# Pinning ScalarE's splits of the experts' weights in the order of use, in a two-layer hybrid encoder

## The chip, the cores and the metric

The kernel runs on one core of a Trainium2 chip. The metric is the device time of one execution in microseconds; the median of three runs is compared.

## What is computed

Two encoder layers work on 256 tokens of width 1024. Each layer has a token mixer (three parallel head groups behind one input projection), a cross-attention into 256 memory tokens, and a channel mixer; each is followed by a residual and a layer norm. The channel mixer of layer 0 is a dense SwiGLU. That of layer 1 is a mixture of 8 experts, of which each token takes 2:

```python
def moe_swiglu(x, w_router, w_gate, w_up, w_down):
    logits = (xt @ w_router)
    top_logit, top_e = lax.top_k(logits, TOP_K)          # 2 of 8
    top_w = jax.nn.softmax(top_logit, axis=-1)
    ...
    def expert_block(args):
        xs, e = args
        hdn = jax.nn.silu(xs @ w_gate[e]) * (xs @ w_up[e])   # 1024 -> 3584
        return hdn @ w_down[e]                               # 3584 -> 1024
```

All is float32. The experts' weights are 8 x 3 x 1024 x 3584 floats, 352 MB, and every one of them is read once.

## The kernel before

**A load and its splits.** `wload` (L293) fetches one piece of a weight matrix, 128 x 2048 floats or 1 MB, by one DMA on SP's queue into a raw tile `wr`. Then it splits the piece for exact products in a faster format: ScalarE copies it, rounded, to `wh` (L313), and VectorE subtracts, `wl = wr - wh` (L317). Both work in two parts of 128 x 1024. In layer 1's experts nothing of this goes to GpSimd. Raw tiles come from a ring of nine buffers, `wh` and `wl` from a ring of four: the split of a load must wait until TensorE is done with the load four before it, and the DMA of a load until TensorE and VectorE are done with the one nine before it.

**An expert in chunks.** `expert_run` (L1367) goes through the eight experts, and for each through seven chunks of 512 hidden columns. A chunk takes six loads. In the program's order these are gate halves g0 and g1 and up halves u0 and u1 (`gate_up`), and then the two down halves d0 and d1 of the chunk before (`flush`, `down`). I write g0 to d1 for them in what follows. TensorE's work on a chunk is: the gate product, four transposes of the hidden tile of the chunk before (`ps_hT`, L1430), the up product, and the two down products into `ps_ye`.

**Two ways to multiply.** `products` (L1372) branches on how many tokens the expert has. Over 64 tokens it runs `passes`: three matmuls a tile, `wh` and `wl` against the split activations (L1377 to L1379). Up to 64 it runs `paired`: one float32 matmul a tile, straight from the raw tile `wr` (L1385), with 64 rows for each of two tiles, which are added up by one more matmul, the fold (L1402). The fold takes `fe`, ScalarE's copy of the product's bank (L1401): the fold of up stands behind the down products, ahead of the next chunk's gate product. The branch is taken on the chip, so the splits are made for every expert, and are read only by those that run `passes`. In the trace these are experts 0, 6 and 7; experts 1 to 5 run `paired`. A matmul block of either way keeps its `wh` and `wl` until the block ends.

**ScalarE's other work in a chunk.** `fe` for gate and for up, the silu `hs` (L1423; VectorE multiplies it with up, L1424, and TensorE transposes it), and from the transposes `hw` (L1434) and `hh` (L409); VectorE makes `hl` (L409). Once an expert there are the gather of the next expert's tokens (`rows`, `xg`, `gw`) and the combine of the finished one (`yh` on ScalarE, `yl` and the sums into `x` on VectorE).

**What sets the order.** No order is written down for the engines. A scheduler takes the program, simulates it, and fixes the order of each engine's instructions from when they could start in that simulation and from priorities; `wload` gives its splits a priority of their own. Each engine then runs its instructions strictly in that order, and an instruction that waits holds up all that stand behind it.

Of the kernel before, what the change touches and what calls it, by code (L numbers as in the profile page):

```python
# [14 lines left out]
AF = mybir.ActivationFunctionType  # L15
# [137 lines left out]
def _offsets():  # L153
    out = {}
    for name, tiles in _tiles().items():
        at = 0
        for t in tiles:
            out[(name,) + t] = at
            at += P * t[2] * t[4]
    return out  # L160
# [3 lines left out]
def tile_encoder(ctx: ExitStack, tc: tile.TileContext, a: dict, out: bass.AP, cw: dict):  # L164
    nc = tc.nc
    V, A, G, T, SY = nc.vector, nc.scalar, nc.gpsimd, nc.tensor, nc.sync
# [28 lines left out]
    def rotate(ring):  # L195
        ring.append(ring.pop(0))
        return ring[-1]
# [92 lines left out]

    where = _offsets()

    def wload(name, i, k0, n0, c0, n1, late=(), whole=False):  # L293

        n = n0 * n1
        W = rotate(parts)
        raw = rotate(raws).tile([P, 2048], F32, name="wr")
        at = where[name, i, k0, n0, c0, n1]
        last_load[:] = [SY.dma_start(raw[:, :n], a[name][at:at + P * n].rearrange("(p n) -> p n", p=P))]
        h = W.tile([P, 2048], F32R, name="wh")  # L300
        l = W.tile([P, 2048], F32R, name="wl")
        c = n // pieces[0]

        if not late and gate[0] <= 0 < gate[0] + GATED:
            late = ln_end
        gate[0] -= 1
        with ExitStack() as es:
            for i in late:
                es.enter_context(tc.issue_after(i.ins))
            es.enter_context(tc.high_priority(offset=WP if in_mixer[0] else WQ))  # L310
            g = n * (GQ - GP[layer[0]]) // GQ if in_mixer[0] else n
            for s in (slice(j, j + c) for j in range(0, n, c)):
                A.activation(h[:, s], raw[:, s], AF.Copy)  # L313
                s0, s1 = s.start, s.stop
                if s0 < g:
                    m = slice(s0, min(s1, g))
                    V.tensor_sub(l[:, m], raw[:, m], R_(h[:, m]))  # L317
                if s1 > g:
                    m = slice(max(s0, g), s1)
                    G.tensor_sub(l[:, m], raw[:, m], R_(h[:, m]))  # L320
        v = lambda t: t[:, :n].rearrange("p (a b) -> p a b", a=n0)
        return (v(h), v(l), v(raw)) if whole else (v(h), v(l))
# [114 lines left out]
    def mixer(l, xh, xl, kctx):  # L437
        wi = ("w_in", l)
        with tc.tile_pool(name=f"mx{l}", bufs=1, reuse_waits="tile") as M, ExitStack() as mctx:
# [323 lines left out]
            if l == 0:  # L763
                next(pf)
                load_first()
            run(pf)
            wh, wl = wload(*wi, 0, KT, 4 * AW, 24)
            pb = bank(psb, "pb", "ps_bd")
            for k in range(KT):
# [855 lines left out]
```

## Time and profile before

| | us |
|---|---|
| median of 3 runs (lowest, highest) | 1989.45 (1986.8, 1990.65) |
| the profiled execution | 1993.32 |
| its span (first to last instruction) | 1991.5 |
| from the silu of expert 0's first chunk to that of expert 1's | 959.9 to 1089.7 |
| the same for experts 1 to 5, 35 chunks | 1089.7 to 1699.6 |
| the same for experts 6 and 7, to the last silu | 1699.6 to 1957.4 |

The profile is one execution. For each engine it gives busy time and idle time and, for the idle time, what ended it. A group's name reads out<-in by the program's names, after the engine and the line. The windows view cuts the span into stretches and gives busy time and number of instructions of each engine, then the clock granted to TensorE as a share of full speed, the busy share of the 16 DMA engines and the rate in GB/s. A silu (L1423) marks a chunk: from one to the next is a chunk's period.

### The profile page before, as it was taken

Reading aid. Unit: us, or ns where it says so; the run is one execution under the profiler, and the core shown is the slowest. Engines: PE = TensorE matmul, PEld = TensorE weight load, DVE = VectorE, ACT = ScalarE, POOL = GpSimd, SP = SyncE. Lnnn points to the kernel's source line nnn. Section 1 sums busy time; section 2 is a strip of 40 time slices with the busy share of each in tenths; the row PEclk is TensorE's granted clock in tenths of the full one; section 3 lists DMA queues with packets and bytes.
Section 4 is the critical chain, followed back from the end, with each engine's and each line's share of the span. In section 5 each row is a group of like instructions: output and inputs, shape, how many; then the busy total and the mean of one; then the engine's idle time right before and its main releaser. Section 6 shows DMA issues by size and latency. Waiting matters only on the chain. (4 is left out here: it accounts for less than half of the span.)

```text
span 1991.5 us, 29272 instructions
## 1 busy us (share of the span) xinstructions
PE 1739.0 (87%) x11084; PEld 1221.9 (61%) x11084; DVE 1551.0 (78%) x2175; ACT 1294.4 (65%) x2071; POOL 258.3 (13%) x248
## 2 busy tenths in 40 slices
PE   6889999999969889996999888888888888998985
PEld 5768778899967677785776333332333334676764
DVE  6887665755488866656778989999998889878775
ACT  4755444555437644453778887888988788777673
POOL 4545210000045452101000000000000000000000
PEclk8988999999989879997999999999999989999998
DMA  6321345555323221650789998999999899888782
GB/s 214 111 97 66 110 179 199 184 181 188 116 75 126 85 100 65 254 192 20 293 318 348 388 347 337 376 366 374 375 380 362 320 359 369 336 310 331 277 304 84
DMA packets 71281, 473.76 MB, mean 238 GB/s; under 512 B 8768, under 2 KB 12224, under 8 KB 15936
## 3 DMA queue, kind: packets, MB, share of 16 engines
q1 hardware_dynamic: 70384, 466.09, 62.9%
q10 hardware_dynamic: 720, 5.24, 0.7%
q8 instruction: 119, 1.95, 0.4%
q14 instruction: 58, 0.48, 0.1%
HBM read 470.26 MB, written 1.05 MB: 237 GB/s over the span
## 5 line engine op out<-in xcount | busy, mean ns | idle before, releaser
L317 DVE TENSOR_TENSOR wl<-wr,wh 128x1024 fp32r<-128x1024 f32 (+3 forms) x950 | 975.4, 1077 | 142.2 <-ACT wh L313 137.2
L313 ACT ACTIVATE wh<-wr 128x1024 fp32r<-128x1024 f32 (+2 forms) x984 | 852.8, 937 | 150.6 <-PE ps_ye L1379 48.1
L1385 PE MATMUL ps_gu<-wr,gw 128*64 128x512 f32 x1120 | 291.3, 631 | 0.1
L1385 PEld LDWEIGHTS ps_gu<-wr,gw 128*64 128x64 f32 x1120 | 95.9, 144 | 150.3 <-issue 142.8
L1402 PE MATMUL ps_gu<-fe,fold 128*64 128x512 f32 x146 | 88.1, 688 | 70.3 <-ACT fe L1401 70.3
L1385 PE MATMUL ps_ye<-wr,hw 128*64 128x512 f32 x560 | 148.2, 596 | 0.1
L1378 PE MATMUL ps_gu<-wl,xg 128*128 128x512 f32 x336 | 134.4, 400 | 11.3 <-DVE wl L317 11.3
L1377 PE MATMUL ps_gu<-wh,xg 128*128 128x512 f32 x336 | 137.1, 408 | 8.2 <-DVE m L1311 5.1
L320 POOL TENSOR_TENSOR wl<-wr,wh 128x384 fp32r<-128x384 f32 (+6 forms) x68 | 103.7, 1544 | 291.3 <-ACT wh L313 290.9
L1549 POOL TENSOR_TENSOR x<-x,lp 128x512 f32<-128x512 f32 x1 | 1.8, 1819 | 1058.8 <-ACT x L1548 1058.8
L1379 PE MATMUL ps_gu<-wh,xg 128*128 128x512 f32 x336 | 133.5, 397 | 0.0
L1434 ACT ACTIVATE hw<-ps_hT 128x512 f32<-128x512 f32 x56 | 33.5, 598 | 117.4 <-PE ps_hT L1430 117.4
L1258 PE MATMUL ps_gu<-xTl,wh 128*128 128x256 f32 x352 | 99.0, 281 | 0.0
L1259 PE MATMUL ps_gu<-xTh,wl 128*128 128x256 f32 x352 | 98.8, 281 | 0.0
L1257 PE MATMUL ps_gu<-xTh,wh 128*128 128x256 f32 x352 | 98.7, 282 | 0.0
L1402 PEld LDWEIGHTS ps_gu<-fe,fold 128*64 128x64 f32 x146 | 16.2, 145 | 125.7 <-ACT fe L1401 117.4
L1385 PEld LDWEIGHTS ps_ye<-wr,hw 128*64 128x64 f32 x560 | 49.9, 136 | 69.9 <-issue 66.7
L1377 PEld LDWEIGHTS ps_gu<-wh,xg 128*128 128x128 f32 x336 | 64.7, 192 | 28.1 <-ACT wh L313 7.4
L1378 PEld LDWEIGHTS ps_gu<-wl,xg 128*128 128x128 f32 x336 | 64.6, 192 | 27.6 <-DVE wl L317 14.5
L1379 PEld LDWEIGHTS ps_gu<-wh,xg 128*128 128x128 f32 x336 | 64.5, 192 | 14.2
L1377 PE MATMUL ps_ye<-wh,hh 128*128 128x512 f32 x168 | 67.5, 402 | 3.9 <-ACT wh L313 3.3
L409 DVE TENSOR_TENSOR hl<-ps_hT,hh 128x512 fp32r<-128x512 f32 x56 | 38.5, 688 | 39.0 <-ACT hh L409 38.8
(469 smaller groups left out, 3744.9 us busy)
## 6 DMA issues: line engine op xcount, KB each, us to landing
wr<-in_moe_wg_dram SPq DMA_DIRECT2D x112, 1024.0 KB, 7.3
wr<-in_moe_wu_dram SPq DMA_DIRECT2D x112, 1024.0 KB, 7.7
wr<-in_moe_wd_dram SPq DMA_DIRECT2D x112, 1024.0 KB, 7.6
wr<-in_w_in_dram SPq DMA_DIRECT2D x16, 1024.0 KB, 4.9
wr<-in_ffn_wg_dram SPq DMA_DIRECT2D x11, 1024.0 KB, 4.9
wr<-in_ffn_wu_dram SPq DMA_DIRECT2D x11, 1024.0 KB, 4.9
wr<-in_ffn_wd_dram SPq DMA_DIRECT2D x11, 1024.0 KB, 4.9
wr<-in_xk_dram SPq DMA_DIRECT2D x8, 1024.0 KB, 4.9
```

The costliest lines, as they stand in the source:

```text
L313: A.activation(h[:, s], raw[:, s], AF.Copy)
L317: V.tensor_sub(l[:, m], raw[:, m], R_(h[:, m]))
L320: G.tensor_sub(l[:, m], raw[:, m], R_(h[:, m]))
L409: return A.activation(h, ps, AF.Copy), V.tensor_sub(l, ps, R_(h))
L1257: T.matmul(ps[:, g], wh[:, k, fs], xh[:, k, :], start=k == 0, stop=False)
L1258: T.matmul(ps[:, g], wh[:, k, fs], xl[:, k, :], start=False, stop=False)
L1259: T.matmul(ps[:, g], wl[:, k, fs], xh[:, k, :], start=False, stop=k == KT - 1)
L1377: T.matmul(out, h[:, k], wh, start=b, stop=False)
L1378: T.matmul(out, h[:, k], wl, start=False, stop=False)
L1379: T.matmul(out, l[:, k], wh, start=False, stop=z)
L1385: T.matmul(out[f * HALF:f * HALF + HALF], hw[:, k, :HALF], w, start=ws[j][5], stop=ws[j + 1][6], skip_group_check=True)
L1402: return lambda: T.matmul(pt[:HALF], fold[e], fe, start=False, stop=True, skip_group_check=True)
```

## The change

`wload` gets a helper, `in_turn`. For the loads of the experts (`whole=True`) it ties each ScalarE part of a split to the part before it, in the order in which the program makes them. The tie is one between two instructions of one engine, so it carries no semaphore: it only forbids the scheduler another order.

```diff
+    split = []
+
+    def in_turn(i):
+
+        if split:
+            tc.add_manual_dep(i.ins, split[-1].ins.name, mybir.DependencyInfo(
+                mybir.DependencyClass.NoSync, mybir.DependencyReason.DATA), reason="in_turn")
+        split[:] = [i]
...
             for s in (slice(j, j + c) for j in range(0, n, c)):
-                A.activation(h[:, s], raw[:, s], AF.Copy)
+                act_i = A.activation(h[:, s], raw[:, s], AF.Copy)
+                if whole:
+                    in_turn(act_i)
```

Up to the experts all engines' orders are the same as before, and so are all instructions in number and kind. In 40 of the 56 chunks ScalarE split u0 ahead of g0 before, and in 14 right behind g0; now it stands behind g1 in all. Lines behind the helper are 9 to 11 further down in the changed kernel (L313 is L322, L1401 is L1412).

ScalarE in the third chunk of expert 1 (the place of rows 4 below), from the split of the second down half, 11566, to the next `hw`; 11596 and 11604 are g0 and g1 of the fourth chunk, 11648 and 11656 its u0 and u1, `fe_11528` and `hs_11592` are the third chunk's copy of up and its silu. Before:

```order
L313 ACTIVATE wh_11568<-wr_11566 128x1024 x2
L1393 UNCONDITIONAL_BRANCH x2
L313 ACTIVATE wh_11650<-wr_11648 128x1024 x2
L313 ACTIVATE wh_11598<-wr_11596 128x1024 x2
L1401 ACTIVATE fe_11528<-ps_gu_11477 128x512
L1423 ACTIVATE hs_11592<-ps_gu_11425 128x512
L313 ACTIVATE wh_11606<-wr_11604 128x1024 x2
L1393 UNCONDITIONAL_BRANCH x2
L313 ACTIVATE wh_11658<-wr_11656 128x1024 x2
L1434 ACTIVATE hw_11705<-ps_hT_11700 128x512
```

Now:

```order
L322 ACTIVATE wh_11568<-wr_11566 128x1024 x2
L1404 UNCONDITIONAL_BRANCH x2
L322 ACTIVATE wh_11598<-wr_11596 128x1024 x2
L1412 ACTIVATE fe_11528<-ps_gu_11477 128x512
L1434 ACTIVATE hs_11592<-ps_gu_11425 128x512
L322 ACTIVATE wh_11606<-wr_11604 128x1024 x2
L322 ACTIVATE wh_11650<-wr_11648 128x1024 x2
L1404 UNCONDITIONAL_BRANCH x2
L322 ACTIVATE wh_11658<-wr_11656 128x1024 x2
L1445 ACTIVATE hw_11705<-ps_hT_11700 128x512
```

The split of u0 moved from ahead of g0, `fe` and the silu to behind g1, so `fe` stands behind one split and not two.

VectorE at the same place, from g0 or u0 to the down half d0 (11711). Before:

```order
L317 TENSOR_TENSOR wl_11651<-wr_11648,wh_11650 128x1024 x2
L317 TENSOR_TENSOR wl_11599<-wr_11596,wh_11598 128x1024 x2
L1393 UNCONDITIONAL_BRANCH
L317 TENSOR_TENSOR wl_11607<-wr_11604,wh_11606 128x1024 x2
L1393 UNCONDITIONAL_BRANCH
L1424 TENSOR_TENSOR hs_11592<-hs_11592,ps_gu_11477 128x512
L317 TENSOR_TENSOR wl_11659<-wr_11656,wh_11658 128x1024 x2
L409 TENSOR_TENSOR hl_11708<-ps_hT_11700,hh_11707 128x512
```

Now:

```order
L328 TENSOR_TENSOR wl_11599<-wr_11596,wh_11598 128x1024 x2
L1404 UNCONDITIONAL_BRANCH
L328 TENSOR_TENSOR wl_11607<-wr_11604,wh_11606 128x1024 x2
L328 TENSOR_TENSOR wl_11651<-wr_11648,wh_11650 128x1024
L1404 UNCONDITIONAL_BRANCH
L328 TENSOR_TENSOR wl_11651<-wr_11648,wh_11650 128x1024
L1435 TENSOR_TENSOR hs_11592<-hs_11592,ps_gu_11477 128x512
L328 TENSOR_TENSOR wl_11659<-wr_11656,wh_11658 128x1024 x2
L420 TENSOR_TENSOR hl_11708<-ps_hT_11700,hh_11707 128x512
```

The subtractions follow ScalarE's new order; the multiplication of the silu stands behind the same six of them as before.

ScalarE at the end of expert 1, where its result is scaled (`yh_12501`, `yh_12513`) before the next expert's first chunk (g0 12530, u0 12582, u1 12590). Before:

```order
L313 ACTIVATE wh_12584<-wr_12582 128x1024 x2
L313 ACTIVATE wh_12532<-wr_12530 128x1024 x2
L1472 ACTIVATE yh_12501<-ps_ye_11358,gs_12497 128x512
L1472 ACTIVATE yh_12513<-ps_ye_11359,gs_12497 128x512
L313 ACTIVATE wh_12592<-wr_12590 128x1024 x2
L1401 ACTIVATE fe_12424<-ps_gu_12373 128x512
L1423 ACTIVATE hs_12526<-ps_gu_12321 128x512
```

Now:

```order
L322 ACTIVATE wh_12532<-wr_12530 128x1024 x2
L1483 ACTIVATE yh_12501<-ps_ye_11358,gs_12497 128x512
L1483 ACTIVATE yh_12513<-ps_ye_11359,gs_12497 128x512
L1412 ACTIVATE fe_12424<-ps_gu_12373 128x512
L1434 ACTIVATE hs_12526<-ps_gu_12321 128x512
```

Both up splits moved behind the silu here. Beside this, three smaller things move. The split of d0 stands ahead of `hw` and `hh` in 31 chunks now, in 9 before. On TensorE, eight chunks had the first down product ahead of the up product; it stands behind it now, as in all others. On SP's queue eight pairs of gate loads and one pair of down loads change places with each other.

## Rows read from the trace of the kernel before

**Rows 1.** The page's first lines: span, busy time and share of each engine.

```profile
span 1991.5 us, 29272 instructions
...
PE 1739.0 (87%) x11084; PEld 1221.9 (61%) x11084; DVE 1551.0 (78%) x2175; ACT 1294.4 (65%) x2071; POOL 258.3 (13%) x248
```

**Rows 2.** Windows of the expert stages; after the engines: granted clock, DMA share, GB/s.

```profile
core 0: us, PE busy (x) PEld busy (x) DVE busy (x) ACT busy (x) POOL busy (x), PEclk, DMA share, GB/s
...
959.90:1089.70 129.80, 120.27 (x517) 92.19 (x518) 103.30 (x99) 98.61 (x124) 0.00 (x0) 0.96 0.85 319
1089.70:1699.60 609.90, 516.57 (x2125) 201.28 (x2125) 559.47 (x561) 510.83 (x646) 0.00 (x0) 0.96 0.95 363
1699.60:1957.40 257.80, 236.65 (x1016) 185.56 (x1015) 205.01 (x199) 185.57 (x231) 0.00 (x0) 0.98 0.81 304
```

**Rows 3.** Waits in 1090 to 1700 us: waiter, releaser, total us, times, longest.

```profile
PE ps_gu L1402 <- ACT fe L1401: 70.3, 35, 2.8
...
DVE wl L317 <- ACT wh L313: 26.8, 51, 1.4
...
ACT wh L313 <- PE ps_ye L1385: 24.5, 23, 1.7
```

**Rows 4.** Timeline of ScalarE in expert 1: start, length, instruction, idle before.

```profile
1116.88 2.01 ACT L313 ACTIVATE wh<-wr 128x1024 fp32r<-128x1024 f32 x2
1119.90 3.90 ACT L313 ACTIVATE wh<-wr 128x1024 fp32r<-128x1024 f32 x4 [1.00 <-PE ps_ye L1385]
1123.70 0.58 ACT L1401 ACTIVATE fe<-ps_gu 128x512 f32<-128x512 f32 x1
1124.18 0.58 ACT L1423 ACTIVATE hs<-ps_gu 128x512 f32<-128x512 f32 x1
1124.65 3.89 ACT L313 ACTIVATE wh<-wr 128x1024 fp32r<-128x1024 f32 x4
1129.46 0.60 ACT L1434 ACTIVATE hw<-ps_hT 128x512 f32<-128x512 f32 x1 [0.92 <-PE ps_hT L1430]
```

**Rows 5.** Timeline of TensorE's matmuls at the same place.

```profile
1117.44 0.64 PE L1385 MATMUL ps_ye<-wr,hw 128*64 128x512 f32 x1
...
1117.92 3.64 PE L1385 MATMUL ps_ye<-wr,hw 128*64 128x512 f32 x15
1124.33 1.07 PE L1402 MATMUL ps_gu<-fe,fold 128*64 128x512 f32 x2 [2.77 <-ACT fe L1401]
1124.84 3.99 PE L1385 MATMUL ps_gu<-wr,gw 128*64 128x512 f32 x16
1128.76 0.66 PE L1430 MATMUL ps_hT<-consts,hs 128*128 128x128 f32 x4
1129.35 3.65 PE L1385 MATMUL ps_gu<-wr,gw 128*64 128x512 f32 x16
```

**Rows 6.** Timeline of VectorE at the same place.

```profile
1115.60 4.74 DVE L317 TENSOR_TENSOR wl<-wr,wh 128x1024 fp32r<-128x1024 f32 x4
1120.98 7.12 DVE L317 TENSOR_TENSOR wl<-wr,wh 128x1024 fp32r<-128x1024 f32 x6 [0.65 <-ACT wh L313]
1128.02 0.68 DVE L1424 TENSOR_TENSOR hs<-hs,ps_gu 128x512 f32<-128x512 f32 x1
```

**Rows 7.** Windows of single chunks, from silu to silu; columns as in rows 2.

```profile
1124.18:1140.10 15.92, 13.15 (x56) 4.90 (x56) 15.13 (x15) 14.00 (x19) 0.00 (x0) 0.99 1.00 399
...
1176.76:1194.40 17.64, 14.85 (x56) 5.92 (x56) 15.30 (x15) 14.03 (x19) 0.00 (x0) 0.90 0.94 352
...
1266.80:1281.60 14.80, 13.88 (x60) 5.16 (x60) 14.66 (x15) 13.88 (x19) 0.00 (x0) 1.00 0.97 374
1281.60:1300.10 18.50, 15.29 (x68) 5.75 (x68) 16.69 (x17) 16.87 (x24) 0.00 (x0) 1.00 0.99 381
...
1739.34:1758.30 18.96, 17.50 (x76) 13.84 (x76) 15.27 (x15) 14.03 (x18) 0.00 (x0) 1.00 0.88 330
```

**Rows 8.** Waits of TensorE in 1699.6 to 1957.4 us; columns as in rows 3.

```profile
PE ps_gu L1378 <- DVE wl L317: 9.1, 8, 1.1
...
PE ps_gu L1377 <- ACT wh L313: 2.5, 8, 0.3
PE ps_ye L1377 <- ACT wh L313: 2.1, 1, 2.1
```

## The prediction, made before the changed kernel was run

> **What bounds the kernel now.** I began with the page's totals: TensorE is busy for 87% of 1991.5 us, VectorE for 78% [rows 1]. Such shares are means over stages, and the change touches one stage only, so the next view was the windows of the three expert stages [rows 2]. Experts 1 to 5, the ones with few tokens, take 609.9 us. There TensorE is busy for 516.6 us, but VectorE for 559.5 us and the DMA engines for 95%. Experts 0 and 6 to 7 are the reverse: TensorE 120.3 of 129.8 us and 236.7 of 257.8 us, with DMA at 85% and 81%. So there are two cases.
>
> The waits of the first case name one culprit [rows 3]: TensorE waited 70.3 us, in 35 waits over 35 chunks, for `fe`, ScalarE's copy of the up product, which the fold needs. The timelines of one chunk show why. TensorE ends the up product and starts the down products at 1117.4; they end at 1117.92 + 3.64 = 1121.6, and then it idles for 2.77 us until `fe` [rows 5]. The up product had been ready for 6 us by then, but ScalarE first sat idle for 1.00 us until TensorE was done with the first down half, then ran four split parts, 3.90 us, and only then `fe` [rows 4]. By the order of ScalarE these four parts are u0 and g0, u0 first. The buffer of u0's split is the one that d0 holds, so u0 waits for the down product, and g0 and `fe` stand behind it though they wait for nothing. This is a ring: up product, first down half, u0, g0, `fe`, fold, gate product, transposes, up product. Its period is 15.92 us in that chunk [rows 7].
>
> VectorE is close behind. In the same chunk it is busy for 15.13 of the 15.92 us [rows 7], and its only idle stretch there is 0.65 us, ahead of the six subtractions that follow the late splits [rows 6]. Over the stage it idled for 609.9 - 559.5 = 50 us, 26.8 of them in waits for splits [rows 2, 3].
>
> **The change part by part.**
>
> *ScalarE's own work* neither grows nor shrinks: the tie adds no instruction and no semaphore.
>
> *u0 behind g0, `fe` and the silu, few tokens.* In the chunk of rows 4, d1's split ends at 1116.88 + 2.01 = 1118.9. g0 needs the buffer of the last chunk's u0, free since 1117.4; so it runs to 1120.9, and `fe` starts there and not at 1123.70. It is done at 1121.5, when the down products end (1121.6): the 2.77 us are gone. TensorE's own ring is then 15.92 - 2.77 = 13.15 us, which is its busy time in that row.
>
> That isn't what a chunk will take, because VectorE needs 15.13 us and ScalarE 14.00. So the bound passes to VectorE, or to the DMA. What is late next is the multiplication of the silu, which still stands behind six subtractions. Two ends for the stage follow. If VectorE keeps the idle time that it has now in an ordinary chunk, 15.92 - 15.13 = 0.79 us, 35 chunks take 559.5 + 28 = 587 us, a gain of 23. If it gets down to that of the chunk at 1266.8, 14.80 - 14.66 = 0.14 us, they take 559.5 + 5 = 564, a gain of 45. That chunk is a preview: there TensorE ran the first down half ahead of the up product, so u0's buffer was free early, and the period was 14.80 us. The DMA gives a third figure. The stage moves 609.9 us x 363 GB/s = 221 MB; at the 381 GB/s that the chunk at 1281.6 shows with a share of 0.99, so at 385 if it were 1.00, this is 575 us, a gain of 35. I take 30: two limits that lie this close are seldom both reached.
>
> Chunks that are longer today give most of it. The one at 1176.8 has the same work, but TensorE's clock was granted at 0.90 over it, it was busy for 14.85 us, and 14.85 + 2.77 gives its 17.64 us [rows 7]. Without the wait such a spell lies under VectorE's 15.3 us: 2 us each. At the ends of experts, where u1 stood ahead of `fe` too, the copy comes another 2 us earlier.
>
> *u0 later, many tokens.* Here TensorE reads the splits. A chunk takes 18.96 us with 17.50 busy [rows 7], and the waits of experts 6 and 7 that splits cause are 9.1 + 2.5 + 2.1 = 13.7 us [rows 8]. They have the same cause: g0 is split behind u0, which waits for the down product's end, so the gate product finds `wl` of g0 unfinished. With g0 free to start when the up product ends, some 5.6 us ahead of its use (the down products lie between, about a third of the chunk's 17.5 us of matmuls), both ScalarE's 2.0 and VectorE's 2.4 us fit in. Expert 0 has the same order; by its idle time, 129.8 - 120.3, I give it a third as much as 6 and 7 together, 5. The bounds are 0 and 19; I take 15, because VectorE's 15.3 and the DMA's 0.88 leave room in a 17.5 us chunk [rows 7].
>
> *What could cost.* u0's split waits for the end of the first down half, and u1, d0, `hw` and the gate's `fe` are queued behind it. From the up product's end, ScalarE reaches u0 after g0, `fe`, the silu and g1, 2.0 + 0.6 + 0.5 + 1.9 = 5.0 us; the first down half ends after about 2.5 us [rows 4, 5]. So it doesn't wait. d0's split now stands ahead of `hw` in 31 chunks: 2.0 us, of which ScalarE has 0.92 us idle at that place [rows 4], and `hw` is wanted only behind the up product, 3.65 us after the transposes [rows 5]. I cost it at nothing; if the cover is gone it is the slower rival below. The eight chunks that lose their early down product lose nothing, since g0 no longer waits for it. The swaps on SP's queue put loads back into the order of use: nothing.
>
> **The sum.** 30 + 15 = 45 us off the profiled execution's 1993.3 gives 1948. The median of the runs is 1989.45, 3.9 us lower, so the forecast is 1944.
>
> **The rivals.**
>
> *The DMA has no more to give.* At 95% busy [rows 2] the stage of few tokens may be at the end of the memory's rate already; then raw tiles land no sooner, TensorE waits for them in place of `fe`, and only the 15 us of the other stage are left: 1974. For it: the share, and a chunk at 381 GB/s with 0.99 [rows 7]. Against it: another chunk ran at 399 [rows 7], which would make 555 us of the stage.
> The Trainium skill (DMA: Bandwidth & Descriptors, section "Where 436 GB/s comes from") states that for transfers between HBM and SBUF the HBM side binds, at about 358 GB/s a core. By that rule the stage, at 363, would be at its end and this rival would hold; the trace speaks against the figure, with 399 GB/s over a chunk.
>
> *VectorE absorbs it.* If the multiplication of the silu comes no earlier, because VectorE works off the same backlog, TensorE waits for it ahead of the transposes and the period stays. For it: 15.13 of 15.92 us in a plain chunk. Against it: the mean period is 609.9 / 35 = 17.4 us, and the mean VectorE time 16.0. Gain about 0 to 3: 1988.
>
> *Slower: `hw` behind d0.* If d0's bytes land later than the transposes, ScalarE waits for them with `hw` queued behind, and the down products with it. It decides when d0's split starts more than about half a microsecond after the transposes (3.65 us of cover, less 2.0 and 1.1 for `hw` and `hh`). Price: 2.0 us in 31 chunks, 62, less the 45 gained: 2006. Against it: the chunk at 1124 had a DMA share of 1.00 [rows 7], and ScalarE waited for TensorE there, not for a landing [rows 4].
>
> **How the numbers follow.** The forecast 0.64, with a range of its own from 1928 (45 + 19 gained) to 1960; the DMA's end 0.19; VectorE absorbs it 0.10; slower 0.07. The range from 1926 to 1978 takes in the forecast and the first rival, and leaves the others out. A measurement of this kernel can tell about 0.2%, 4 us, from no change. Faster by more is 0.64 + 0.19 = 0.83, the same 0.10, slower 0.07.
>
> **What would show it.** Right: TensorE's wait for `fe` falls from 70.3 us to under 15; ScalarE's wait for `ps_ye` ahead of a split, 24.5 us now [rows 3], is gone; VectorE's idle time in the 35 chunks falls from 50 us to 15 to 30; the DMA's rate there rises from 363 to 375 or more; chunks of 18.96 us become 17.5. The DMA rival shows as an unchanged rate at a share of 0.98 or more, the absorbed one as a wait of the transposes for the silu, the slower one as a wait of `ps_ye` for `hw`. The prediction is wrong if ScalarE waits for landings in its new order, since everything behind them then waits too.

## The result, and the profile after

| | us |
|---|---|
| before: median of now four runs (lowest, highest) | 1990.05 (1986.8, 1990.87) |
| after: median (lowest, highest) | 1906.57 (1902.47, 1907.08) |
| ratio, 95% interval | 0.9579 (0.9562 to 0.9596) |
| forecast (range) | 1944 (1926 to 1978) |

The change saves 83.5 us, not the 45 of the forecast. The sign and the place were right, the size was not, and the time lies below the range. The kernel before was measured again on the chip of each experiment; its median lay between 1989.35 and 1991.49 us. In one profiled execution (many_only) TensorE's clock was granted at 0.82 from end to end, so the rows of that kernel come from a second profile, many_only_again.

The page's first lines, which answer to [rows 1]:

```profile
span 1900.7 us, 29392 instructions
...
PE 1708.9 (90%) x11084; PEld 1210.6 (64%) x11084; DVE 1540.7 (81%) x2175; ACT 1293.5 (68%) x2071; POOL 256.9 (14%) x248
```

The windows of the three expert stages, which answer to [rows 2], with the same columns (us, busy time of PE, PEld, DVE, ACT, POOL, granted clock, DMA share, GB/s):

```profile
949.40:1071.20 121.80, 119.35 (x536) 92.05 (x534) 103.57 (x101) 99.44 (x125) 0.00 (x0) 1.00 0.92 354
1071.20:1638.50 567.30, 508.78 (x2124) 199.05 (x2124) 553.17 (x561) 509.87 (x647) 0.00 (x0) 0.95 0.97 389
1638.50:1865.50 227.00, 224.96 (x1007) 182.72 (x1008) 202.62 (x200) 187.05 (x232) 0.00 (x0) 1.00 0.91 346
```

The profiled execution took 1902.47 us, 90.9 less than that of before. By stages: 10.5 up to the first silu (959.9 to 949.4), 8.0 in expert 0, 42.6 in experts 1 to 5, 30.8 in experts 6 and 7, and 1.1 lost behind them. Of the first figure 5.9 us are no gain of the change: they lie ahead of expert 0's first gate product (939.3 us before, 933.4 after), where the orders are the same in both kernels. They come from the choice of executions: the one of before lies 3.3 us above its median, that of after 4.1 below, 7.4 together, and 90.9 - 7.4 is the 83.5 of the medians. The other 4.6 us are a gain in expert 0's first chunk: from its gate product to its silu it took 20.6 us before and takes 16.0 after. The experiments below bear it out: it takes 16.0 us where expert 0 is tied in full (many_only_again) and 20.4 where it isn't tied (few_only) or its down halves are left free (gate_up_only).

The waits in experts 1 to 5, which answer to [rows 3] (waiter, releaser, total us, times, longest):

```profile
PE ps_hT L1441 <- DVE hs L1435: 49.8, 21, 5.4
ACT hw L1445 <- PE ps_hT L1441: 39.3, 20, 3.7
DVE wl L328 <- ACT wh L322: 11.4, 21, 1.1
...
PE ps_gu L1413 <- ACT fe L1412: 2.5, 5, 0.6
```

TensorE's wait for `fe` fell from 70.3 us to 2.5, and ScalarE's waits for `ps_ye` ahead of a split are gone. In their place TensorE waits 49.8 us ahead of the transposes for the silu's product, which comes from VectorE. But VectorE has only 567.3 - 553.2 = 14 us of idle time left in this stage, where it had 50 [rows 2]. It sets the pace now, which quarter_sub tests below.

A pair of ordinary chunks of expert 7 beside the chunk of 18.96 us in [rows 7] (a pair, since the silu comes early and late by turns, 15.3 and 18.6 us apart):

```profile
1782.40:1816.30 33.90, 33.90 (x154) 27.83 (x153) 30.92 (x30) 28.06 (x35) 0.00 (x0) 1.00 0.96 369
```

A chunk takes 16.95 us there, with TensorE busy from end to end. It is half a microsecond less than the 17.50 that the forecast took for TensorE's own work.

### The profile page after: what moved, and what is told of

Same layout as the page of the kernel before. It is cut to its first block, busy times and chain, and to the rows that moved or that the text cites. A ratio compares the mean times of both kernels' runs of the same rounds, so it can differ in the third digit from the quotient of the medians.

```text
span 1900.7 us, 29392 instructions
## 1 busy us (share of the span) xinstructions
PE 1708.9 (90%) x11084; PEld 1210.6 (64%) x11084; DVE 1540.7 (81%) x2175; ACT 1293.5 (68%) x2071; POOL 256.9 (14%) x248
## 5 line engine op out<-in xcount | busy, mean ns | idle before, releaser
L322 ACT ACTIVATE wh<-wr 128x1024 fp32r<-128x1024 f32 (+2 forms) x984 | 846.4, 946 | 74.2 <-PE ps_gu L1269 22.7
L1396 PEld LDWEIGHTS ps_gu<-wr,gw 128*64 128x64 f32 x1120 | 89.6, 145 | 153.3 <-issue 147.8
L1396 PEld LDWEIGHTS ps_ye<-wr,hw 128*64 128x64 f32 x560 | 51.5, 136 | 70.3 <-issue 66.6
L1441 PE MATMUL ps_hT<-consts,hs 128*128 128x128 f32 x224 | 38.3, 297 | 59.7 <-DVE hs L1435 51.4
L1441 PEld LDWEIGHTS ps_hT<-consts,hs 128*128 128x128 f32 x224 | 26.4, 148 | 90.6 <-DVE hs L1435 73.7
L1413 PE MATMUL ps_gu<-fe,fold 128*64 128x512 f32 x146 | 75.5, 598 | 3.4 <-ACT fe L1412 3.4
L1412 ACT ACTIVATE fe<-ps_gu 128x512 f32<-128x512 f32 x112 | 68.2, 609 | 13.3 <-PE ps_gu L1413 8.3
```

What stands on the lines that cost most here:

```text
L322: act_i = A.activation(h[:, s], raw[:, s], AF.Copy)
L1396: T.matmul(out[f * HALF:f * HALF + HALF], hw[:, k, :HALF], w, start=ws[j][5], stop=ws[j + 1][6], skip_group_check=True)
L1412: A.activation(fe, pt, AF.Copy)
L1413: return lambda: T.matmul(pt[:HALF], fold[e], fe, start=False, stop=True, skip_group_check=True)
```

## The experiments

In each diff the changed kernel stands on the minus side. "Theory A" is the explanation that I started from: each stage gains by itself, from the place of u0's split alone.

### Which stage gives what: few_only, many_only, many_only_again

```diff
-                if whole:
+                if whole and 1 <= expert <= 5:        # few_only
+                if whole and expert in (0, 6, 7):     # many_only, many_only_again
                     in_turn(act_i)
```

> The tie only for experts 1 to 5 (few tokens); experts 0, 6 and 7 keep the scheduler's own order. Theory A: each stage gains by itself, and the gains are those between the two profiles, 43 us in experts 1 to 5 and 39 in experts 0, 6 and 7; then this kernel takes about 1947 us (1941 to 1953), its stage of experts 1 to 5 about 567 us, and its plain chunks of experts 0, 6 and 7 stay at 18.9 us. Rival B: the stages gain 30 and 15 as predicted, and the rest of the difference between the two profiles is TensorE's granted clock, which was lower in parts of the profile of before; then about 1960 us. Rival C: the gain of experts 6 and 7 comes from what the loads have reached by the end of expert 5; then the stage of many tokens gets faster here too, and the time is under 1930 us.

> The tie only for experts 0, 6 and 7 (many tokens). Theory A: about 39 us of gain, so 1951 us (1944 to 1958); plain chunks there take 16.9 us and not 18.9, which is TensorE's 72 matmuls at the 0.229 us from start to start that both profiles show, and experts 1 to 5 keep 35 waits for fe and about 70 us in them. Rival B: the prediction's 15 us for this part were right and the rest was clock; then about 1975 us.

> The tie only for experts 0, 6 and 7 once more, for a profile at the usual clock: the first one had a clock of 0.82 from end to end. Theory A: plain chunks of many tokens 16.9 us, the stage of experts 6 and 7 about 227 us, expert 0 about 122 us, experts 1 to 5 as before with 35 waits for fe; about 1951 us, and by the undisturbed runs of the first time 1942 to 1948. What the two parts give by themselves, 49 and 43 us by the first comparison, is more than the 84 us of both; the profile should show in which stage the 8 us lie.

few_only took 1941.39 us, ratio 0.9756 (0.974 to 0.9773); many_only 1947.43, 0.978 (0.9757 to 0.9802), and the second time 1944.74, 0.9762 (0.9731 to 0.9792). Windows of experts 1 to 5, then 6 and 7, first of few_only, then of many_only_again:

```profile
1086.30:1652.60 566.30, 507.35 (x2124) 197.72 (x2124) 553.39 (x561) 510.55 (x648) 0.00 (x0) 0.95 0.97 390
1652.60:1906.20 253.60, 234.91 (x1016) 185.43 (x1015) 205.25 (x199) 185.75 (x231) 0.00 (x0) 0.99 0.82 309
```

```profile
1073.70:1679.60 605.90, 515.25 (x2126) 201.71 (x2124) 558.15 (x560) 508.72 (x645) 0.00 (x0) 0.96 0.95 363
1679.60:1907.10 227.50, 225.32 (x1009) 182.81 (x1008) 203.22 (x200) 187.76 (x233) 0.00 (x0) 1.00 0.91 347
```

Each tie brings its stage to the length that it has in the changed kernel (567.3 and 227.0) and leaves the other some 4 us below that of before (609.9 and 257.8). Rivals B and C are out: the 39 us of the experts with many tokens are no luck of the clock and don't come from what the other stage leaves behind. By the medians the two parts give 49 and 43 to 45 us, 8 to 10 more than both together, and the 4 us by which each untouched stage is shorter make up about as much. In few_only they lie in expert 7: three of its chunks, from transposes to transposes, take 21.94, 16.95 and 16.93 us there and 18.93, 18.96 and 22.14 in the kernel before. The long one of the three is each time the one in which the scheduler has the first down product ahead of the up product, and the chunks behind it run without a break; in few_only it is the first of the three, in the kernel before the last. So a tie in one stage also moves the scheduler's order in the other. In many_only_again ScalarE's order differs from that of before in experts 3 to 5; which chunks its 4 us come from stays open.

### Whether it is u0's place: u0_first, held_same, u0_second

The four loads of gate and up are issued first, in the old order; then their splits are made in a chosen order and tied.

```diff
+ORDER = (2, 0, 1, 3)     # u0_first; (0, 1, 2, 3) held_same; (0, 2, 1, 3) u0_second
...
+                    held = [wload(..., whole=True, hold=True)
+                            for ws in ("moe_wg", "moe_wu") for kh in range(2)]
+                    for j in ORDER:
+                        held[j][3]()      # the split of load j
```

> The tie as in the changed kernel, but in the order u0, g0, g1, u1 in every chunk; the four loads are issued in the old order, ahead of the splits. Theory A: the place of u0's split ahead of g0 is the whole cause, since it waits for the down product and holds up g0 and fe; then TensorE's wait for fe comes back in all 35 chunks of experts 1 to 5 with 2 to 3 us each, chunks of many tokens are back at about 18.9 us, and the time is about that of before or somewhat above it, 1985 to 2010 us. Rival D: it is the fixed order as such, or the six loads of a chunk in step with it, that helps (no load overtakes another), whichever comes first; then 1907 to 1930 us.

> The same rewriting as u0_first, four loads issued ahead of the splits, but with the splits in the order g0, g1, u0, u1, so ScalarE's order is that of the changed kernel. All theories: the rewriting itself costs nothing, 1907 us (1903 to 1911). If it is slower than that, u0_first has to be read against this kernel and not against the changed one.

held_same took 1905.3 us, ratio 0.9572 (0.9556 to 0.9589): the rewriting costs nothing. u0_first took 2029.71, ratio 1.0192 (1.0161 to 1.0223). So the tie as such doesn't help: the same tie with u0 in front is slower than no tie. Its window and its main waits in experts 1 to 5, and one plain chunk:

```profile
1098.40:1736.70 638.30, 534.46 (x2124) 210.16 (x2124) 561.79 (x561) 512.05 (x646) 0.00 (x0) 0.93 0.91 346
...
1623.30:1640.70 17.40, 14.66 (x56) 5.05 (x56) 15.54 (x15) 13.98 (x19) 0.00 (x0) 0.90 0.95 358
```

```profile
PE ps_gu L1419 <- ACT fe L1418: 89.6, 40, 2.8
...
ACT wh L324 <- PE ps_ye L1402: 43.5, 35, 2.3
```

The wait for `fe` is back, 2.77 us in a plain chunk, as in [rows 5], and so is ScalarE's wait for the down product. I had expected 1985 to 2010 us. What I left out is that the chunk isn't 15.92 us long with this wait in it but 17.4: the granted clock over it is 0.90, and the same work takes TensorE 14.66 us in place of 13.15. It is the second kind of chunk in [rows 7], the one of 17.64 us. With a break in every chunk most of them are of this kind. Plain chunks of many tokens are back at 18.88 to 18.96 us, as theory A says. Beside the 28 us that experts 1 to 5 take more than in before, expert 0 takes 14 more (144.1 against 129.8), which the expectation had no term for.

> As held_same (1905 us), but with the splits in the order g0, u0, g1, u1. By the scheduler's order u0 is then behind g0 but still ahead of fe and the silu. Theory A has two effects of u0's place, and this parts them. For TensorE's gate product in experts 0, 6 and 7 only g0 is urgent; g1, wanted 2.8 us later, has time, so plain chunks stay at 16.9 us, or 17.5 at most. For fe in experts 1 to 5 u0 still stands in front and waits for the first down half: fe comes 4 us after that half's end in before's order and 2 to 3 here, so a wait for fe of 1 to 2 us a chunk comes back, 35 to 70 us in sum, part of it under VectorE; the stage takes 580 to 600 us and not 567 to 571, and the kernel 1920 to 1940. If only 'u0 ahead of g0' mattered, it would take 1905.

u0_second took 1905.93 us, ratio 0.958 (0.9564 to 0.9596), as fast as the changed kernel. My expectation of 1920 to 1940 was wrong, in an instructive way. Its window, one chunk, and its largest wait of TensorE:

```profile
1073.30:1637.60 564.30, 500.19 (x2124) 194.27 (x2124) 553.44 (x560) 508.22 (x647) 0.00 (x0) 0.99 0.98 392
...
1218.50:1233.40 14.90, 13.21 (x56) 4.53 (x56) 14.88 (x15) 13.82 (x18) 0.00 (x0) 1.00 0.99 406
```

```profile
PE ps_gu L1419 <- ACT fe L1418: 52.4, 40, 1.7
```

TensorE does wait for `fe` again, 52.4 us in sum, and it costs nothing. With g0's split, 2.0 us, out of it I estimate the ring of TensorE at 15.92 - 2.0 = 13.9 us; VectorE is busy for 14.88 us of the 14.90 in that chunk and sets its length. TensorE's idle time only moved, from the transposes to the fold. By this reading what cost time in before was not the wait but a ring that was longer than VectorE's work. So u0's place counts only as u0 *ahead of g0*.

### What bounds experts 1 to 5 now: quarter_sub

```diff
-                    m = slice(s0, min(s1, g))
+                    m = slice(s0, s0 + 256 if whole and 1 <= expert <= 5 else min(s1, g))
```

> The changed kernel, but in experts 1 to 5 VectorE subtracts only 256 of each 1024 columns of a split part; nobody reads the rest there, since these experts multiply straight from the raw tiles. This leaves some 350 us of VectorE's work out of that stage. Theory E: VectorE, busy for 553 of 567 us there, is what bounds the stage now; the next limits are the DMA, 220 MB at the 420 GB/s of its fastest chunks, 525 us, and ScalarE's and TensorE's 510; so the stage takes 525 to 540 us and the kernel 1865 to 1880. Rival F: the DMA, busy for 97% there, is at its end already; then nothing moves, 1900 to 1910. Chunks of experts 0, 6 and 7 stay at 16.9 us by both.

It took 1868.48 us, ratio 0.938 (0.9355 to 0.9405), inside the expectation of theory E. The stage, and one plain chunk of it:

```profile
1075.50:1604.10 528.60, 495.64 (x2129) 187.89 (x2129) 259.06 (x562) 506.95 (x648) 0.00 (x0) 0.99 1.01 418
...
1406.10:1419.80 13.70, 12.90 (x57) 4.67 (x56) 6.24 (x15) 13.70 (x18) 0.00 (x0) 1.00 1.01 419
```

VectorE does bound the stage in the changed kernel: without some 290 us of its work the stage is 39 us shorter. And the DMA can do more than the forecast allowed it: 418 GB/s over 528 us, with 1.01 as the share. At that rate the 221 MB take 529 us. Whether that is the DMA's end isn't shown, since ScalarE is full too: it is busy for all 13.70 us of the plain chunk, and over the stage it waited for landings for 1.5 us only. The forecast had read the end off a chunk with 381 GB/s and a share of 0.99 [rows 7]; a share near 1 is no sign that the rate is at its end.
The Trainium skill (DMA: Bandwidth & Descriptors, section "Where 436 GB/s comes from") states that the HBM side binds at about 358 GB/s a core; this run shows 418 on one core, and the measurement decides.

### Two ways to relieve VectorE that fail: pool_two, one_piece

```diff
             g = n * (GQ - GP[layer[0]]) // GQ if in_mixer[0] else n
+            if name == "moe_wu" and k0 == 4 or name == "moe_wd" and k0 % 4 == 2:
+                g = n // 2                  # pool_two: the second part goes to GpSimd
-        c = n // pieces[0]
+        c = n if whole else n // pieces[0]  # one_piece
```

> The changed kernel with two of the twelve subtractions of a chunk on GpSimd, the second part of u1 and of d1. Nothing is left out. In the profile of the changed kernel a subtraction of 128x1024 takes GpSimd 2.48 us and VectorE 1.18, so VectorE's load falls by 2.4 us a chunk, from 15.8 to 13.4 on the mean. Theory E (VectorE bounds experts 1 to 5): a chunk there takes about 15.0 us, where the DMA at 420 GB/s or ScalarE come next, and the kernel 1870 to 1885. Rival F (the DMA is at its end): 1900 to 1910. A third way: the later subtraction on GpSimd holds up the products of experts 0, 6 and 7, which read it; 21 chunks with 1 us each would give back 20 of the gain. If those are bound by TensorE alone, they stay at 16.9 us.

pool_two took 1957.69 us, ratio 0.983 (0.9808 to 0.9853), 51 us slower than the changed kernel; in its profile experts 1 to 5 take 613.5 us. Its subtractions on VectorE and on GpSimd (count, busy time, mean ns of one), and one place of the timelines of VectorE and GpSimd:

```profile
L330 DVE TENSOR_TENSOR wl<-wr,wh 128x1024 fp32r<-128x1024 f32 x560 | 827.1, 1526 | 42.7 <-ACT wh L324 42.6
...
L333 POOL TENSOR_TENSOR wl<-wr,wh 128x1024 fp32r<-128x1024 f32 x130 | 371.3, 2856 | 686.8 <-ACT wh L324 558.6 <-DVE wl L330 68.8 <-PE ps_gu L1391 24.4
```

```profile
1211.26 3.25 DVE L330 TENSOR_TENSOR wl<-wr,wh 128x1024 fp32r<-128x1024 f32 x1
...
1211.05 2.38 POOL L333 TENSOR_TENSOR wl<-wr,wh 128x1024 fp32r<-128x1024 f32 x1 [1.99 <-ACT wh L324]
```

VectorE has 112 subtractions less, but the 560 that it keeps take 1526 ns on the mean and not 1219: 172 us more, for 137 saved. In the timeline one takes 3.25 us while GpSimd runs its own. Sorted by whether a GpSimd instruction lies beside them, 205 of the 350 in experts 1 to 5 have none and take 1.21 us, and 129 overlap one in part and take 2.10 on the mean, the longest 3.43. Of these, 69 begin within a GpSimd subtraction and outlast it, and each ends 1.08 us behind it. The other 16 lie wholly within one and take 1.21; there the GpSimd one takes 3.49 or 6.3 us. So whichever begins second waits. The work wasn't shared, it stood in line.
The Trainium skill (SBUF — State Buffer, section "SBUF: two separate sides") states that an operation of VectorE with two inputs in SBUF and a GpSimd operation that reads SBUF exclude each other for a whole instruction; these rows agree. I should have weighed that before I expected a gain.

> The changed kernel, but each split of the experts' weights is one copy and one subtraction of 128x2048, not two of 128x1024. In the profile of the changed kernel a row of ten subtractions takes 11.44 us, 1.14 each, and by the 0.699 us of 512 columns and the 1.219 of 1024 the columns alone cost 1.04 us a piece; so VectorE is spared some 0.1 us six times a chunk, about 20 us in experts 1 to 5, and ScalarE more. Theory E (VectorE bounds that stage): 545 to 555 us there and 1885 to 1895 in all. Against it: coarser pieces let VectorE start 1 us later behind each copy, and if experts 0, 6 and 7 wait for wl again, 21 chunks with 0.5 to 1 us give it back, 1895 to 1910. quarter_sub showed that this stage has 39 us to give where VectorE has less to do.

one_piece took 1927.08 us, ratio 0.968 (0.9663 to 0.9697), 20 slower than the changed kernel. Experts 1 to 5, then 6 and 7:

```profile
1072.70:1654.10 581.40, 505.45 (x2125) 197.13 (x2124) 543.22 (x350) 490.50 (x436) 0.00 (x0) 0.96 0.96 379
1654.10:1892.10 238.00, 230.94 (x1015) 186.72 (x1014) 199.08 (x123) 180.12 (x155) 0.00 (x0) 0.98 0.87 332
```

VectorE's busy time in experts 1 to 5 did fall, from 553 to 543 us, but its idle time rose from 14 to 38. Most of the rise, 17 us, is waiting for the copy ahead of a subtraction (28.3 us against 11.4), which is one of 128x2048 now. Experts 6 and 7 lost 11 us. The expectation looked at the work only, not at the grain of the hand-over.

### The smaller steps: hh_first, gate_up_only

```diff
                     ends = evac_split(hh, hl, pT)
+                    in_turn(ends[0])                      # hh_first
-                if whole:
+                if whole and name != "moe_wd":            # gate_up_only
                     in_turn(act_i)
```

> The changed kernel, but hh is tied into the same chain behind u1, so hw and hh stand ahead of d0's split in all 56 chunks; in the changed kernel d0 stands ahead of them in 31. It tests the rival of the prediction that went to the slower side, at a price of 2.0 us in each of these chunks. If d0's split ahead of hw costs something now, this is faster by up to 62 us. The prediction costed it at nothing, since that split lies in ScalarE's idle time; then the time is within 5 us of 1907, or somewhat above it, where d0's split comes later by the wait for the transposes and VectorE behind it.

> The tie for gate and up alone; the splits of the down halves are free, as before the change. By theory A the down halves have no share in the gain: 1907 us (1902 to 1912). A share of theirs would show as a time above 1912.

gate_up_only took 1907.61 us, ratio 0.9588 (0.9572 to 0.9604): the down halves have no share that the time shows. In its profile expert 0's first chunk alone is as long as in the kernel before. hh_first took 1920.55, ratio 0.9652 (0.9626 to 0.9679), 14 slower than the changed kernel. In its profile, the fastest of its four executions, experts 1 to 5 take 575.3 us, 8 more, and 4.4 more lie behind the last silu (39.6 us against 35.2):

```profile
1070.60:1645.90 575.30, 511.55 (x2126) 195.91 (x2124) 557.95 (x562) 510.23 (x648) 0.00 (x0) 0.96 0.96 384
```

So d0's split ahead of `hw` isn't a price but worth a little. The likely reason, which no run shows by itself, is that ScalarE fills with it time that it would spend waiting for the transposes.

### The ends of the experts: y_first, skip_load, skip_load_y

A plain chunk explains about 2 us of gain, and eight of the thirteen chunks of experts 6 and 7 are plain. From one chunk's transposes to the next one's they took 18.89 to 18.96 us before and 16.93 to 17.00 after, 16 us in sum. The chunk at the end of expert 6 went from 26.9 to 21.7. skip_load came upon these ends by accident: it skips, by a branch on the chip, the subtractions that experts with few tokens never read, which is what quarter_sub recommends.

```diff
+                with tc.If(needed > HALF):     # skip_load; needed: VectorE's copy of the expert's count
+                    for s in cuts:
+                        V.tensor_sub(l[:, s], raw[:, s], R_(h[:, s]))
...
+                for y in scaled:               # skip_load_y: both yh behind the next chunk's g0
+                    tc.add_manual_dep(y.ins, split[-1].ins.name, ...)
...
-                        A.activation(yh, ye[n], AF.Copy, scale=gs)
+                        in_turn(A.activation(yh, ye[n], AF.Copy, scale=gs))     # y_first
```

> The changed kernel with a branch on VectorE around the two subtractions of each load of the experts, on the same count of tokens that TensorE branches on: experts that multiply from the raw tiles skip them. Nothing that is read is left out. By quarter_sub and theory E, experts 1 to 5 get to 525 to 535 us, where the DMA at 420 GB/s is the end, and the kernel to 1866 to 1885. Against it: no trace here shows what a branch costs VectorE; there are six a chunk, and an engine that has to fetch its instructions anew might lose 1 us at each. In experts 1 to 5 VectorE has room for that (it would have about 2 us of work in a chunk). In experts 0, 6 and 7 it is busy for 15.3 of 16.9 us, and 21 chunks with six branches of 0.5 us each would give back some 21 x 1.4 = 29 us: about 1900. A branch also parts the two subtractions of a load from what the scheduler put between them.

skip_load took 1907.03 us, ratio 0.9576 (0.956 to 0.9592), like the changed kernel: experts 1 to 5 went down to 537.1 us, but experts 6 and 7 up from 227.0 to 248.4 and expert 0 from 121.8 to 129.3.

```profile
955.60:1084.90 129.30, 123.83 (x540) 93.98 (x538) 93.22 (x92) 100.03 (x126) 0.00 (x0) 0.97 0.91 350
1084.90:1622.00 537.10, 500.18 (x2125) 189.74 (x2124) 91.52 (x149) 505.41 (x646) 0.00 (x0) 0.98 1.00 409
1622.00:1870.40 248.40, 234.78 (x1012) 188.12 (x1011) 204.42 (x201) 189.12 (x232) 0.00 (x0) 0.97 0.82 312
```

Its plain chunks stayed at 16.93 us, so six branches a chunk on VectorE cost nothing that shows. The loss lay at the ends of experts. There the scheduler had put one of the two `yh`, which wait for the last down product, ahead of g0's split. It had also changed TensorE's order at these places: in the last chunk of expert 6 and in the one behind it the first down product stands ahead of the up product, where it stands behind it in the changed kernel.

> The changed kernel with the two yh of an expert's end tied into the chain, so they stand ahead of the next chunk's g0 and not behind it. Theory G: the loss at the ends of experts in the kernel before was of the same kind as that of plain chunks: on ScalarE, g0 stood behind something that waits for the last down product. There it was u0 (and u1 ahead of fe), here it is yh; so the chunk at the end of expert 6, 26.9 us before and 21.7 after, gets to 25 to 29 us, and the one at the end of expert 0, 20.1 before, to 20 to 24. In experts 1 to 5 VectorE hides it, up to 2 us at each of five ends. Sum 10 to 20 us, 1917 to 1927. Rival H: the ends of experts were long in before because of u1 alone, or because of a lower granted clock by chance; then 1905 to 1911.

y_first took 1927.08 us, ratio 0.9685 (0.9669 to 0.9701), 20.5 slower than the changed kernel, as theory G says. Experts 6 and 7, and the two chunks that follow an expert's end:

```profile
1648.90:1889.90 241.00, 230.39 (x1010) 186.12 (x1010) 204.40 (x199) 188.17 (x232) 0.00 (x0) 0.98 0.84 323
...
1654.80:1680.00 25.20, 25.17 (x100) 20.58 (x101) 22.23 (x22) 16.89 (x20) 0.00 (x0) 0.88 0.64 236
1789.90:1813.90 24.00, 24.00 (x100) 19.61 (x101) 20.59 (x19) 15.00 (x18) 0.00 (x0) 0.93 0.64 244
```

The stage is 14.0 us longer than in the changed kernel, 7 us for each of the two ends, so rival H is out. But the two chunks don't show the loss by themselves. From transposes to transposes they took 17.1 and 16.9 us in the changed kernel, with 77 matmuls in them and not 100: in y_first TensorE has the transposes ahead of the gate product and not behind it, so each stretch holds one product of 24 matmuls more, some 5.5 us at 0.229 us a step. What is lost lies in a wait of TensorE just ahead of each stretch:

```profile
PE ps_hT L1441 <- DVE hs L1435: 4.5, 1, 4.5
...
PE ps_hT L1441 <- DVE hs L1435: 4.1, 1, 4.1
```

Behind the wait some ten matmuls come 0.43 us apart and not 0.23, which is most of the rest: the clock was granted at 0.88 and 0.93 over the stretches, and at 1.00 over the stage of the changed kernel. So a `yh` ahead of g0 does cost the stage, as theory G says. That it does so in the way of u0 in a plain chunk isn't shown, since TensorE's order changed with it.

> skip_load (VectorE branches past the subtractions that nobody reads) with both yh tied behind the next chunk's g0, as they stand in the changed kernel; in skip_load one of them stood ahead of it. Theory G: skip_load's loss of 29 us in experts 0, 6 and 7 lies at the ends of experts and comes from that yh, not from the branches (its plain chunks stayed at 16.9 us); then the ends are back at 19 to 22 us, experts 1 to 5 stay at 530 to 537, and the kernel takes 1872 to 1885, less than both kernels of the case. Rival I: the branches or the loads (which come in bunches where a stage is at the DMA's end) cost it there; then 1895 to 1907 again.

skip_load_y took 1892.52 us, ratio 0.9515 (0.9495 to 0.9535). It beats both kernels of the case, by 14 us the changed one, but misses the 1872 to 1885 that I expected. Experts 1 to 5, experts 6 and 7, and the chunk at the end of expert 6:

```profile
1079.10:1610.70 531.60, 494.44 (x2126) 187.75 (x2127) 93.28 (x151) 507.27 (x647) 0.00 (x0) 0.99 1.01 414
1610.70:1854.00 243.30, 233.76 (x1008) 187.54 (x1007) 203.30 (x200) 189.26 (x233) 0.00 (x0) 0.96 0.85 323
...
1728.70:1756.40 27.70, 24.82 (x94) 18.07 (x93) 17.14 (x21) 13.73 (x19) 0.00 (x0) 0.88 0.64 246
```

The place of `yh` was worth 14.5 us by the medians (12 by the ratios): 8 of the 29 that skip_load had lost in experts 0, 6 and 7, and most of the rest in experts 1 to 5. The other 21 are still lost at the ends of experts. In this chunk the loss begins with three breaks of TensorE, 2.5 us in sum, for `gs`, for a split and for `hl`, after which matmuls come 0.43 us apart for twelve or so and not 0.23; the granted clock is 0.50 from 1733.6 to 1738.5 us, TensorE's lower level of 1.2 GHz. The breaks fall on the first down product, which stands ahead of the up product here as in skip_load and so wants `hh`, `hl` and its split earlier than in the changed kernel. Which order would remove them wasn't tried.

## Why the prediction was wrong in size

**The mechanism** was right. u0's split ahead of g0 held up `fe` in one stage and the gate product in the other (u0_first, few_only, many_only_again). What counts is u0 ahead of g0, and not u0 ahead of `fe` (u0_second). Of what the prediction named as signs, the wait for `fe` (2.5 us), ScalarE's wait for `ps_ye` (gone) and the DMA's rate (389 GB/s) came as said. VectorE's idle time fell to 14 us, a little under the 15 to 30 forecast, and chunks of 18.96 us became 16.95, not 17.5. One sum was off: 45 + 19 us gained leave 1925 and not 1928.

**Experts 1 to 5: 30 forecast, 42.6 measured,** close to the upper bound of 45. The step that failed is the choice between the bounds. I took 30 because the DMA, at 575 us, and VectorE seemed to be two limits close together. The 575 was wrong: quarter_sub moves the same bytes in 529 us. VectorE alone was the limit, and the stage came within 14 us of its busy time. That busy time fell besides, from 559.5 to 553.2 us, in part because more of its subtractions follow each other in an unbroken row and take less each (eight in 9.16 us after, against 1.22 for a single one).

**Experts 0, 6 and 7: 15 forecast, 38.8 measured,** twice the upper bound of 19, and 43.4 with the 4.6 of expert 0's first chunk. Three readings failed in it.

First, the floor. I took TensorE's 17.50 us of busy time in a chunk of 18.96 for its work. Rows of before at a break (start, length, instruction, idle before), and of after where the gate product follows the down products without one:

```profile
1756.08 0.39 PE L1378 MATMUL ps_ye<-wl,hh 128*128 128x512 f32 x1
1756.31 0.39 PE L1379 MATMUL ps_ye<-wh,hl 128*128 128x512 f32 x1
1757.02 0.50 PE L1377 MATMUL ps_gu<-wh,xg 128*128 128x512 f32 x1 [0.33 <-ACT wh L313]
1758.65 0.51 PE L1378 MATMUL ps_gu<-wl,xg 128*128 128x512 f32 x1 [1.13 <-DVE wl L317]
1759.00 0.40 PE L1379 MATMUL ps_gu<-wh,xg 128*128 128x512 f32 x1
1759.23 0.40 PE L1377 MATMUL ps_gu<-wh,xg 128*128 128x512 f32 x1
```

```profile
1802.31 0.39 PE L1390 MATMUL ps_ye<-wh,hl 128*128 128x512 f32 x1
1802.54 0.40 PE L1388 MATMUL ps_gu<-wh,xg 128*128 128x512 f32 x1
1802.78 0.40 PE L1389 MATMUL ps_gu<-wl,xg 128*128 128x512 f32 x1
1803.01 0.39 PE L1390 MATMUL ps_gu<-wh,xg 128*128 128x512 f32 x1
```

A matmul is listed with 0.39 us, but in a row they start 0.23 us apart: they overlap. At a break the overlap is lost, and part of what it costs is listed as busy. From 1756.31 to 1759.00 three steps take 2.69 us in place of 3 x 0.23; so the break costs 2.0 us, where the idle time says 0.33 + 1.13 = 1.46. At 0.229 us, the mean of 38 such steps of after up to 1691.86, the 72 matmuls take 16.49 us; the four transposes add 0.45 (from 1790.87 to 1792.01 three steps with the transposes between them take 1.14 us and not 0.69). That makes a floor of 16.94 us, and a chunk after takes 16.95.
The Trainium skill (Perfetto Trace Analysis, the note at its head) calls matmul busy time a bad metric for how close a kernel is to roofline, because matmuls are pipelined; these rows agree, with 17.50 us of busy time listed for work that takes 16.95 without a break.

Second, the sum. I added up the waits for splits in the table, 13.7 us for experts 6 and 7 [rows 8]. By chunks the gain is 27.7 us from the first transposes of that stage to the last: 16 in eight plain chunks, 5.2 at the end of expert 6, 5.2 in the chunk of 22.1 us (now 16.9), and 1.6 in the chunk with the gather (0.2 are lost in the first). The chunk of 22.1 us is one of the eight in which TensorE had the first down product ahead of the up product, and of which I expected nothing but that they lose nothing. It holds the single wait of 2.1 us in the table, and that one was for d0's split and not for g0's.

Third, the ends of experts and the clock had no term at all. In before the clock was granted at 0.87 over the chunk at the end of expert 6 and at 0.92 over the one of 22.1 us; after, it is 1.00 over the stage. Breaks and the lower clock went together in u0_first and y_first too. How the 10.4 us of the chunks of 26.9 and 22.1 us part between fewer breaks and a better clock wasn't separated.

**The rest.** `hw` behind d0, costed at nothing with a rival of 62 us, is worth 14 us the other way by the medians (hh_first). The DMA rival is out (418 GB/s in quarter_sub). "VectorE absorbs it" was half right: the wait that it named, of the transposes for the silu's product, did come, 49.8 us of it, but at a period 1.2 us shorter on the mean (609.9 / 35 against 567.3 / 35). By stages the change gives 4.6 + 8.0 + 42.6 + 30.8 - 1.1 = 84.9 us, and the medians say 83.5; so the gain lies in the two stages that the prediction named, and its terms for both were too small.

## What to carry to other kernels

Find the ring before the wait: a wait costs only as far as its ring is longer than the work of the busiest engine, so 70 us of waiting for `fe` were worth 43 here, and 52 us of the same wait in another order were worth nothing. Where an engine's instructions overlap, take its floor from the starts in an unbroken row, not from busy time, and count a break from start to start. In an in-order queue, keep what waits for the end of a phase behind everything that the next phase needs first, and look at the ends of the outer loop by themselves.

## What the runs showed of the hardware

- VectorE and GpSimd subtracted SBUF tiles by turns and not side by side (pool_two): 1.21 us on VectorE alone, 2.10 on the mean and up to 3.43 where a GpSimd subtraction (2.86 us on the mean, 2.48 in the kernel before) overlaps in part; all 69 that began within one and outlasted it ended 1.08 us behind it.
- One core's DMA held 418 GB/s over 528 us (quarter_sub). Chunks with a share of 0.99 to 1.01 had rates from 381 to 419 GB/s.
- A branch on VectorE around each pair of subtractions, six a chunk, left chunks of 16.93 us at 16.93 (skip_load).
- TensorE's granted clock over experts 1 to 5 was 0.96 before and 0.95 in the changed kernel (waits of up to 5.4 us), 0.93 in u0_first (40 waits for `fe` of up to 2.8 us) and 0.99 in u0_second (40 of up to 1.7 us).
